# Up-projections of three feed-forward parts by seven products of halves in place of eight

## The chip, the cores and the metric

One core of one Trainium2 chip runs the kernel. The metric is the device time of one execution in microseconds (us), as the median of several runs. TensorE (PE) multiplies matrices, VectorE (DVE) and ScalarE (ACT) work on whole tiles, GpSimd (POOL) does smaller parts, and SyncE (SP) issues the transfers from memory.

## The reference

512 tokens of 1024 features pass through two blocks: a mixer of two attention branches, attention over a memory of 256 tokens, a feed-forward part with a gelu (stage ffa); then a retention part (ret), a feed-forward part with a silu (ffb), a stick-breaking attention (stk) and another feed-forward part (ffc). Each part adds to x. The change touches the feed-forward parts, all of width 2816:

```python
def conv_ffn(h, w_up, conv_w, conv_b, w_down):            # ffa
    u, g = jnp.split(h @ w_up, 2, axis=-1)
    u_pad = jnp.pad(u, ((0, 0), (CONV_WIDTH - 1, 0), (0, 0)))
    u = sum(conv_w[tap] * u_pad[:, tap:tap + S] for tap in range(CONV_WIDTH)) + conv_b
    return (jax.nn.gelu(u) * g) @ w_down

def _conv_ffn(h, w_up, conv_w, conv_b, w_down):           # ffb, ffc
    u = h @ w_up
    u = ...                       # the same causal convolution of width 3, over all 2 * 2816 columns
    gate, val = jnp.split(u, 2, axis=-1)
    return (jax.nn.silu(gate) * val) @ w_down

x = x + conv_ffn(rms_norm(x, ln_ffn_g), w_up, conv_w, conv_b, w_down)
```

## The kernel before

Activations lie transposed: x is eight tiles of 128 features x 512 tokens, all in SBUF. Every float32 factor is split into a high and a low part (`split`: ACT rounds the high part at L148, DVE subtracts to get the low one at L149), and a product is three matmuls, high by high, low by high, high by low (`mm3`, L175 to L177).

A feed-forward part (`ffn`) first scales and splits x (`norm_x`); the norm's factor of each token, rB, is applied when a product is read out of PSUM. Then come three blocks of 8, 8 and 6 pairs (`FF_PARTS`). A pair j is one u unit (columns j of the first half of w_up) and one g unit (the same columns of the second half). A unit is 128 output features: 1024 columns of weights, eight slices of 128 features with three matmuls of 512 tokens each, added up in one PSUM bank "pp" of six. `wload` fetches a unit by one DMA of 512 KB into one of two raw buffers wr and splits it into wh and wl, of which there are three each.

For each pair DVE reads u out of PSUM with the factor rB (L841), a convolution of three taps follows (ACT at L827, DVE at L828 and L829), ACT applies gelu or silu, DVE reads g (L846 in ffa; L852 in ffb and ffc, which convolve g too), multiplies (L847 or L854) and splits the result into mid (L855). After the pairs of a block, the down-projection of that block (`out_proj`, 24 matmuls a unit) adds eight tiles to x (L298), and in the last block of ffc `down_halves` does part of it by halves of the tokens, 256 columns a matmul, and the final norm.

Buffers of a stage come from a pool that the stage opens: 12 buffers wk of 512 columns for temporaries, 20 of mid. The library that records the kernel orders each engine's queue by a plan of its own; on the chip each engine runs its queue strictly in that order, and an instruction that waits holds up all behind it on its engine.

Of the kernel before, what the change touches and what calls it, by code (L numbers as in the profile page):

```python
# [65 lines left out]
def tile_blocks(ctx: ExitStack, tc: tile.TileContext, a: dict, out: bass.AP, dbg=None):  # L66
# [50 lines left out]


# [194 lines left out]
    def mixer():  # L313
        iw = a["w_in_fm"]
        keep = ExitStack()
        kp = sbpool("mix", keep)
        with stage("gla", {"pp": 4, "pa": 3, "ss": 1}, 5) as st:
# [32 lines left out]
            gl = sm.tile([P, NT, 24], F32, name="gl", bufs=1)  # L350
            al = sm.tile([P, NT, 16], F32, name="al", bufs=1)
# [8 lines left out]
            gates = sm.tile([P, NT, 24], F32, name="gates", bufs=1)  # L360
# [35 lines left out]
            for f in range(2):  # L396
# [219 lines left out]
        with stage("nsa", {"pp": 2, "s": 3, "pt": 2, "po": 1}, 2) as st:  # L616
# [52 lines left out]
            def values(kv, i, prs):  # L669
# [5 lines left out]
                for x, (b, o, n, v) in enumerate(blocks):  # L675
# [154 lines left out]

    def ffn(st, gname, up, down, second=None):
        h, rcol, rB, ahead = norm_x(gname, [a[up][i] for i in (0, NF, 1)])

        def up_unit(i):
            return ahead.pop(0) if ahead else fm_unit(wload(a[up][i]), h, KD)

        for part, (j0, nj) in enumerate(FF_PARTS):
            mid = []
            for j in range(j0, j0 + nj):
                u, y = wkt(), wkt()  # L840
                dve.tensor_mul(u, up_unit(j), rB)  # L841
                if second is None:
                    conv(y, u, "conv_w", "conv_b", NF, j)
                    act.activation(y, y, AF.Gelu_apprx_tanh)
                    g = wkt()
                    dve.tensor_mul(g, up_unit(NF + j), rB)  # L846
                    dve.tensor_mul(y, y, g)  # L847
                else:
                    conv(y, u, f"conv_w{second}", f"conv_b{second}", 2 * NF, j)
                    act.activation(y, y, AF.Silu)  # L850
                    u2, y2 = wkt(), wkt()
                    dve.tensor_mul(u2, up_unit(NF + j), rB)  # L852
                    conv(y2, u2, f"conv_w{second}", f"conv_b{second}", 2 * NF, NF + j)
                    dve.tensor_mul(y, y, y2)  # L854
                mid.append(split_new(y, st, "mid", 20))  # L855
# [4 lines left out]
    def down_halves(st, name, mid):  # L860
# [5 lines left out]
        us = [wload(a[name][m], tiles(st, "wd", 2, 2 * NHALF, F32R, w)) for m in range(m0, KD)]  # L866
# [7 lines left out]
        def finish(half, mid=None):  # L874
# [313 lines left out]
    with stage("ffa", {"pp": 6, "pa": 2}, 12) as st:  # L1188
        ffn(st, "ln_ffn", "w_up", "w_down")
# [4 lines left out]
    with stage("ffb", {"pp": 6, "pa": 2}, 12) as st:  # L1194
        ffn(st, "ffn_norm0", "up0", "down0", second=0)
# [4 lines left out]
    with stage("ffc", {"pp": 6, "pa": 2}, 12) as st:  # L1200
        ffn(st, "ffn_norm1", "up1", "down1", second=1)
# [149 lines left out]
```

## Time and profile before

| | |
|---|---|
| median of 3 runs | 2341.67 us (2338.39 to 2344.12) |
| the profiled execution, its span | 2338.12 us, 2336.3 us |
| granted TensorE clock, mean | 0.994 of full speed |
| PE busy (matmuls) | 2294.6 us, 98% of the span, 10872 |
| DVE busy | 1398.4 us, 60%, 2194 |
| ACT busy | 1021.6 us, 44%, 1662 |
| POOL busy | 194.0 us, 8%, 228 |
| one high part of a unit on ACT (L148, 128x1024) | 1044 ns on average |
| one high part of mid on ACT (L148, 128x512) | 631 ns on average |
| one weight unit from issue to landing | 3.2 us (median) |

The up-projection blocks, from the first u read out of PSUM (first block) or the last addition of the down-projection before (second and third) to the first addition of the block's own down-projection, in us from the trace:

| stage | first block, 8 pairs | second, 8 pairs | third, 6 pairs |
|---|---|---|---|
| ffa | 75.2 | 92.7 | 69.7 |
| ffb | 76.1 | 93.5 | 71.6 |
| ffc | 76.1 | 93.6 | 71.6 |

Busy time is a share of the span over stages with different limits. A matmul's own duration (some 0.39 us) is longer than the distance at which matmuls follow one another, since they overlap; a matmul's price is that distance. The same holds in a lesser degree on DVE.

### The profile page before, as it was taken

How to read it: one execution, taken by the hardware profiler on the slowest of the kernel's cores; microseconds unless marked ns; L12 is line 12 of the kernel's file. 1: busy time of each engine (PE TensorE's matmuls, PEld its weight loads, DVE VectorE, ACT ScalarE, POOL GpSimd, SP SyncE). 2: the span in 40 equal slices, each digit the busy share in tenths (PEclk: the TensorE clock that was granted, in tenths of full speed). 3: DMA queues.
4: the chain of work that ended last, by engine and by line, in shares of the span. 5: the costliest groups of instructions: out<-in, count | busy, mean ns of one | idle time of the engine just before them, and what ended most of it. 6: DMA issues, size and time to landing. Idle time of an engine off the chain costs nothing.

```text
span 2336.3 us, 28002 instructions
## 1 busy us (share of the span) xinstructions
PE 2294.6 (98%) x10872; PEld 1881.3 (81%) x10872; DVE 1398.4 (60%) x2194; ACT 1021.6 (44%) x1662; POOL 194.0 (8%) x228
## 2 busy tenths in 40 slices
PE   8999999999999999999999999999999999999997
PEld 7787778878888888888887788888888887888886
DVE  5457875457545356545454674746577886747465
ACT  4345763444323234423323442424477884424243
POOL 2001110101000003000000100000121101000002
PEclk9999999999999999999999999999999999999998
DMA  4221032312222223222222232222344322222222
GB/s 159 91 64 54 28 118 98 115 66 100 99 91 99 95 90 113 82 91 81 81 90 73 81 108 90 99 92 93 98 118 105 91 64 81 99 98 92 99 92 71
DMA packets 66054, 213.41 MB, mean 91 GB/s; under 512 B 7793, under 2 KB 10114, under 8 KB 65794
## 3 DMA queue, kind: packets, MB, share of 16 engines
q1 hardware_dynamic: 60802, 203.24, 26.2%
q0 software_dynamic: 5120, 8.39, 1.7%
q8 instruction: 85, 1.39, 0.2%
q14 instruction: 47, 0.39, 0.1%
HBM read 201.11 MB, written 2.10 MB: 87 GB/s over the span
## 4 chain that ended last, share of the span: by engine, by line
PE 91%; DVE 4%; ACT 2%; issue 1%; POOL 1%; DMA 0%; SPq 0%; DVEq 0%; POOLq 0%; ACTq 0%
PE pp L176 26%; PE pp L175 26%; PE pp L177 26%; PE po L682 1%; DVE wl L149 1%; DVE xl L268 1%; PE pt L678 1%; ACT pr L654 1%; PE po L1143 1%; PE pp L1050 1%; PE pp L1052 1%; PE pp L1051 1%; POOL pr L663 1%; DVE x L298 1%; PE pa L982 1%
## 5 line engine op out<-in xcount | busy, mean ns | idle before, releaser
L148 ACT ACTIVATE wh<-wr 128x1024 fp32r<-128x1024 f32 (+2 forms) x368 | 384.3, 1044 | 790.4 <-PE pp L176 623.2
L175 PE MATMUL pp<-xh,wh 128*128 128x512 f32 x1612 | 634.9, 394 | 3.0 <-ACT xh L267 2.8
L176 PE MATMUL pp<-xl,wh 128*128 128x512 f32 x1612 | 631.8, 392 | 3.6 <-DVE xl L268 3.6
L177 PE MATMUL pp<-xh,wl 128*128 128x512 f32 x1612 | 632.0, 392 | 0.0
L149 DVE TENSOR_TENSOR wl<-wr,wh 128x1024 fp32r<-128x1024 f32 (+2 forms) x368 | 452.4, 1229 | 209.3 <-ACT wh L148 182.8
L175 PEld LDWEIGHTS pp<-xh,wh 128*128 128x128 f32 x1612 | 303.8, 189 | 66.8 <-ACT xh L267 4.1
L176 PEld LDWEIGHTS pp<-xl,wh 128*128 128x128 f32 x1612 | 303.9, 189 | 66.3 <-DVE xl L268 5.5
L177 PEld LDWEIGHTS pp<-xh,wl 128*128 128x128 f32 x1612 | 303.7, 188 | 62.7 <-issue 0.9
L298 DVE TENSOR_TENSOR x<-x,pp 128x512 f32<-128x512 f32 x130 | 89.2, 686 | 244.4 <-PE pp L177 244.3
L175 PE MATMUL pp<-mid,wh 128*128 128x512 f32 x504 | 198.9, 396 | 0.0
L176 PE MATMUL pp<-mid,wh 128*128 128x512 f32 x504 | 198.6, 395 | 0.0
L177 PE MATMUL pp<-mid,wl 128*128 128x512 f32 x504 | 198.5, 395 | 0.0
L237 POOL TENSOR_TENSOR acc<-acc 128x512 f32<-128x512 f32 (+1 forms) x60 | 80.4, 1340 | 913.0 <-ACT acc L233 839.1
L176 PE MATMUL pp<-wl,xh 128*128 128x512 f32 (+1 forms) x320 | 122.3, 382 | 4.0 <-DVE wl L149 4.0
L175 PE MATMUL pp<-wh,xh 128*128 128x512 f32 (+1 forms) x320 | 121.4, 381 | 0.8 <-ACT wh L148 0.8
L177 PE MATMUL pp<-wh,xl 128*128 128x512 f32 (+1 forms) x320 | 121.3, 380 | 0.0
L175 PEld LDWEIGHTS pp<-mid,wh 128*128 128x128 f32 x504 | 94.4, 187 | 24.8 <-ACT mid L148 2.0
L176 PEld LDWEIGHTS pp<-mid,wh 128*128 128x128 f32 x504 | 94.4, 187 | 23.7 <-DVE mid L149 0.9
L177 PEld LDWEIGHTS pp<-mid,wl 128*128 128x128 f32 x504 | 94.4, 187 | 22.8
L148 ACT ACTIVATE mid<-wk 128x512 fp32r<-128x512 f32 x66 | 41.5, 631 | 124.4 <-DVE wk L854 108.8
L827 ACT ACTIVATE wk<-wk,vec 128x512 f32<-128x512 f32 x110 | 88.6, 809 | 6.5 <-DVE wk L841 5.2
L829 DVE SCALAR_TENSOR_TENSOR wk<-wk,vec 128x510 f32<-128x510 f32 x110 | 82.3, 750 | 3.6
(426 smaller groups left out, 3369.3 us busy)
## 6 DMA issues: line engine op xcount, KB each, us to landing
wr<-in_up SPq DMA_DIRECT2D x88, 512.0 KB, 3.2
wr<-in_w_up SPq DMA_DIRECT2D x44, 512.0 KB, 3.2
wr<-in_w_in_fm SPq DMA_DIRECT2D x32, 512.0 KB, 3.6
wr<-in_ret_vg SPq DMA_DIRECT2D x32, 512.0 KB, 3.2
wr<-in_down SPq DMA_DIRECT2D x32, 512.0 KB, 3.2
wr<-in_w_down SPq DMA_DIRECT2D x16, 512.0 KB, 3.2
wr<-in_ret_qk SPq DMA_DIRECT2D x16, 512.0 KB, 3.3
wr<-in_ret_out SPq DMA_DIRECT2D x16, 512.0 KB, 3.3
```

Source lines behind the costliest of these rows:

```text
L148: act.activation(hi, src, AF.Copy)
L149: dve.tensor_sub(lo, src, hi.bitcast(F32))
L175: pe.matmul(ps, sh, mh, start=first and i == 0, stop=False)
L176: pe.matmul(ps, sh, ml, start=False, stop=False)
L177: pe.matmul(ps, sl, mh, start=False, stop=last and i == n - 1)
L237: (dve if k == len(tiles) - 1 else pool).tensor_add(acc[:, :n], acc[:, :n], sq[:, :n])
L268: dve.scalar_tensor_tensor(lo, x, g, hi.bitcast(F32), op0=OP.mult, op1=OP.subtract)
L298: dve.tensor_add(xT[m], xT[m], ps)
L654: act.activation(dst, dst, AF.Exp, scale=-1.0, bias=nm[:, b:b + 1], accum_out=ss[:, g, b:b + 1])
L663: scaler(b).tensor_scalar(prs[g][b], prs[g][b], ss[:, g, b:b + 1], 1.0, op0=OP.mult, op1=OP.mult)
L827: act.activation(dst, src, AF.Identity, scale=V(wname, 2 * nw + j), bias=V(bname, j))
L829: dve.scalar_tensor_tensor(dst[:, 2:], src[:, :S - 2], V(wname, j), dst[:, 2:], op0=OP.mult, op1=OP.add)
```

## The change

Of each pair's 1024 x 256 weights and 1024 x 512 activations, the columns of weights (u and g), the features (first and second four slices) and the tokens (first and second 256) are halved. In place of eight products of halves, four for u and four for g, seven products of sums of halves are formed, each of 4 x 3 matmuls with 256 columns, and the results are put together from them. The first two pairs of each feed-forward part (`NPLAIN`) stay as they were. The sums of activations (t1 to t4) are formed once in a feed-forward part, those of weights (S1, S2, S4 in sa, S3 in the raw buffer of g) for every pair, two of them on POOL. Stage buffers change in size and number, and the pools are laid out with fillers.

```diff
+NPLAIN = 2
+HS = S // 2
...
+    def fill(pool_, n):
+        pool.memset(pool_.tile([P, n], F32, name="fill"), 0.0)
+    fill(sm_, 16)
...
-            gl = sm.tile([P, NT, 24], F32, name="gl", bufs=1)
+            gl = ms.tile([P, NT, 24], F32, name="gl", bufs=1)
...
+            fill(op, 120)
...
+        nrB, = tiles(st, "nrB", 1)
...
+        def plain(j):
+            ug = new_ug(st)
+            dve.tensor_mul(ug[:, 0, :], up_unit(j), rB)
+            dve.tensor_mul(ug[:, 1, :], up_unit(NF + j), rB)
+            return ug, 1.0
+
+        def half_sums():
+            out = []
+            for i in range(2):
+                out.append([st.tile([P, KD // 2, S], F32R, tag="tt", name="tt", bufs=4) for _ in range(2)])
+            for k in range(KD // 2):
+                y1, y2, t1, t2 = [wkt() for _ in range(4)]
+                act.activation(y1, xT[k], AF.Copy, scale=V(gname, k))
+                act.activation(y2, xT[k + 4], AF.Copy, scale=V(gname, k + 4))
+                dve.tensor_sub(t1[:, :HS], y1[:, :HS], y1[:, HS:])
+                dve.tensor_sub(t1[:, HS:], y2[:, HS:], y1[:, HS:])
+                split(out[0][0][:, k, :], out[0][1][:, k, :], t1)
+                dve.scalar_tensor_tensor(t2[:, :HS], t1[:, HS:], -1.0, y1[:, :HS], op0=OP.mult, op1=OP.subtract)
+                dve.scalar_tensor_tensor(t2[:, HS:], t2[:, :HS], -1.0, y2[:, :HS], op0=OP.mult, op1=OP.subtract)
+                split(out[1][0][:, k, :], out[1][1][:, k, :], t2)
...
+        def seven(j, ops):
+            ru, rg = [wpool.tile([P, UNIT], F32, tag="r", name="wr", bufs=NRAW) for _ in range(2)]
+            sync.dma_start(ru, a[up][j])
+            sync.dma_start(rg, a[up][NF + j])
+            k1, k2 = slice(0, S), slice(S, UNIT)
+            sa = st.tile([P, UNIT], F32, tag="sa", name="sa")
+            pool.tensor_add(sa[:, k1], rg[:, k1], rg[:, k2])
+            dve.tensor_add(sa[:, k2], sa[:, k1], ru[:, k1])
+            pool.tensor_add(rg[:, k1], rg[:, k1], ru[:, k1])
...
+            pu = parts(ru)
+            ps_ = parts(sa, st, ("sh", "sl"), 1)
+            dve.tensor_add(sa[:, k2], sa[:, k2], ru[:, k2])
+            pg = parts(rg)
+            p4 = parts(sa[:, k2], st, ("s4h", "s4l"), 1, S)
...
+            pa, pb, pc = [bank("pp")[:, :HS] for _ in range(3)]
...
+            product(pa, pu, 0, "11", True, True)
+            act.activation(g[:, h0], pa, AF.Copy)
+            product(pb, ps_, S, "t2", True, True)
+            dve.tensor_add(u[:, h1], pb, g[:, h0])
+            product(pc, ps_, 0, "t1", True, True)
+            dve.tensor_add(g[:, h1], pc, g[:, h0])
+            product(pa, pu, S, "21", False, True)
+            dve.tensor_mul(u[:, h0], pa, rB[:, h0])
+            product(pb, pg, 0, "t3", False, True)
+            dve.tensor_add(g[:, h1], pb, g[:, h1])
+            product(pc, p4, 0, "22", False, True)
+            dve.tensor_add(u[:, h1], pc, u[:, h1])
+            dve.tensor_mul(u[:, h1], u[:, h1], rB[:, h1])
+            product(pb, pg, S, "t4", False, True)
+            dve.tensor_add(g[:, h0], pb, g[:, h0])
+            dve.tensor_mul(g, g, nrB)
+            return ug
...
-                dve.tensor_mul(u, up_unit(j), rB)
+                    ug = seven(j, ops)
...
-                mid.append(split_new(y, st, "mid", 20))
+                mid.append(split_new(y, st, "mid", 18))
...
-    with stage("ffa", {"pp": 6, "pa": 2}, 12) as st:
+    with stage("ffa", {"pp": 6, "pa": 2}, 7) as st:
```

`parts` splits a source into its high and low part as `split` does; `product` is `mm3` over four slices with 256 columns; `down_halves` uses buffers of tags tt, ug and wk in place of its own.

DVE in the second block of ffb, before: one pair, from the reading of u (L841) to the split of mid (L149, mid). pp is PSUM, wr the raw weights, wh and wl their parts, wk a temporary.

```order
1273 L841 TENSOR_TENSOR wk<-pp,rB 128x512
1274 L149 TENSOR_TENSOR wl<-wr,wh 128x1024
1275 L828 SCALAR_TENSOR_TENSOR wk<-wk,vec 128x511
1276 L829 SCALAR_TENSOR_TENSOR wk<-wk,vec 128x510
1277 L852 TENSOR_TENSOR wk<-pp,rB 128x512
1278 L149 TENSOR_TENSOR wl<-wr,wh 128x1024
1279 L828 SCALAR_TENSOR_TENSOR wk<-wk,vec 128x511
1280 L829 SCALAR_TENSOR_TENSOR wk<-wk,vec 128x510
1281 L854 TENSOR_TENSOR wk<-wk 128x512
1282 L149 TENSOR_TENSOR mid<-wk,mid 128x512
```
DVE in the same block, after: the operations of the first part of a pair's time. ug holds u and g, sa the sums of weights, wsl the low part of S1 and S2; lines are those of the changed kernel, where the split is L157.

```order
1667 L914 TENSOR_TENSOR ug<-pp,ug 128x256
1668 L952 TENSOR_TENSOR wk<-wk 128x512
1669 L916 TENSOR_TENSOR ug<-pp,ug 128x256
1670 L918 TENSOR_TENSOR ug<-pp,rB 128x256
1671 L157 TENSOR_TENSOR mid<-wk,mid 128x512
1672 L920 TENSOR_TENSOR ug<-pp,ug 128x256
1673 L889 TENSOR_TENSOR sa<-sa,wr 128x512
1674 L157 TENSOR_TENSOR wl<-wr,wh 128x1024
1675 L922 TENSOR_TENSOR ug<-pp,ug 128x256
1676 L157 TENSOR_TENSOR wsl<-sa,wsh 128x1024
1677 L923 TENSOR_TENSOR ug<-ug,rB 128x256
1678 L925 TENSOR_TENSOR ug<-pp,ug 128x256
```
And the rest of that pair's time; ws4l is the low part of S4, L838 and L839 are the two convolution steps.

```order
1679 L899 TENSOR_TENSOR sa<-sa,wr 128x512
1680 L926 TENSOR_TENSOR ug<-ug,nrB 128x512
1681 L838 SCALAR_TENSOR_TENSOR wk<-ug,vec,wk 128x511
1682 L157 TENSOR_TENSOR wl<-wr,wh 128x1024
1683 L839 SCALAR_TENSOR_TENSOR wk<-ug,vec,wk 128x510
1684 L838 SCALAR_TENSOR_TENSOR wk<-ug,vec,wk 128x511
1685 L157 TENSOR_TENSOR ws4l<-sa,ws4h 128x512
1686 L839 SCALAR_TENSOR_TENSOR wk<-ug,vec,wk 128x510
```
Ten rows have become twenty: one split of 1024 columns more, the split of ws4l, two sums (L889, L899), seven operations of 256 columns in place of two readings of 512, and the scaling by nrB. The split of mid and the product (L952) belong to the pair before.

POOL at the norms before the memory attention and before ffa, and at the start of ret, before; L237 is the sum of squares of a norm, L210 a power, L904 a product of norm factors in ret.

```order
33 L210 TENSOR_TENSOR y<-v,mhalf 128x2
34 L237 TENSOR_TENSOR acc<-acc 128x512 x6
35 L210 TENSOR_TENSOR y<-v,mhalf 128x4
36 L237 TENSOR_TENSOR acc<-acc 128x512 x6
37 L210 TENSOR_TENSOR y<-v,mhalf 128x4
38 L904 TENSOR_TENSOR g_7095<-vec 128x1
```
POOL at the same two norms, and what follows them, after; L245 and L218 are those two lines now.

```order
36 L245 TENSOR_TENSOR acc<-acc 128x512 x6
37 L218 TENSOR_TENSOR y<-v,mhalf 128x4
38 L245 TENSOR_TENSOR acc<-acc 128x512 x6
39 L218 TENSOR_TENSOR y<-v,mhalf 128x4
40 L888 TENSOR_TENSOR sa<-wr 128x512
41 L890 TENSOR_TENSOR wr<-wr 128x512
42 L888 TENSOR_TENSOR sa<-wr 128x512
```
The norm's rows stand as they did; behind them 20 couples of additions (L888, L890), one for each pair of the new kind, follow in every feed-forward part.

## Rows read from the trace of the kernel before

**Rows 1.** Page, section 4: shares of the chain that ended last
```profile
PE 91%; DVE 4%; ACT 2%; issue 1%; POOL 1%; DMA 0%; SPq 0%; DVEq 0%; POOLq 0%; ACTq 0%
```

**Rows 2.** Windows: start:end, length, busy us (x) PE PEld DVE ACT POOL, PEclk, DMA
```profile
1447.70:1541.20 93.50, 93.50 (x412) 76.97 (x411) 65.65 (x82) 40.23 (x50) 0.00 (x0) 1.00 0.28 96
1579.70:1651.30 71.60, 71.60 (x315) 58.85 (x314) 49.10 (x63) 29.94 (x39) 0.00 (x0) 1.00 0.26 87
```

**Rows 3.** DVE timeline of ffb: start, us, line, operation, [wait <-releaser]
```profile
1332.35 0.68 DVE L841 TENSOR_TENSOR wk<-pp,rB 128x512 f32<-128x512 f32 x1
...
1408.47 0.69 DVE L298 TENSOR_TENSOR x<-x,pp 128x512 f32<-128x512 f32 x1 [0.82 <-PE pp L177]
...
1446.97 0.69 DVE L298 TENSOR_TENSOR x<-x,pp 128x512 f32<-128x512 f32 x1 [3.51 <-PE pp L177]
```

**Rows 4.** PE timeline, up-projection of ffb
```profile
1450.19 0.39 PE L175 MATMUL pp<-xh,wh 128*128 128x512 f32 x1
1450.42 0.39 PE L176 MATMUL pp<-xl,wh 128*128 128x512 f32 x1
```

**Rows 5.** PE timeline, memory projection and last down-projection
```profile
459.60 0.28 PE L175 MATMUL pp<-mm,wh 128*128 128x256 f32 x1
...
460.28 0.28 PE L175 MATMUL pp<-mm,wh 128*128 128x256 f32 x1
...
2301.03 0.39 PE L176 MATMUL pp<-mid,wh 128*128 128x512 f32 x1
...
2301.50 0.28 PE L175 MATMUL pp<-mid,wd 128*128 128x256 f32 x1
...
2302.08 0.28 PE L177 MATMUL pp<-mid,wd 128*128 128x256 f32 x1
...
2302.44 0.28 PE L177 MATMUL pp<-mid,wd 128*128 128x256 f32 x1
```

**Rows 6.** DVE timeline, three places
```profile
558.63 0.75 DVE L829 SCALAR_TENSOR_TENSOR wk<-wk,vec 128x510 f32<-128x510 f32 x1
559.29 0.74 DVE L828 SCALAR_TENSOR_TENSOR wk<-wk,vec 128x511 f32<-128x511 f32 x1
...
1353.36 0.68 DVE L841 TENSOR_TENSOR wk<-pp,rB 128x512 f32<-128x512 f32 x1
1353.96 1.21 DVE L149 TENSOR_TENSOR wl<-wr,wh 128x1024 fp32r<-128x1024 f32 x1
1355.10 0.74 DVE L828 SCALAR_TENSOR_TENSOR wk<-wk,vec 128x511 f32<-128x511 f32 x1
1355.87 0.75 DVE L829 SCALAR_TENSOR_TENSOR wk<-wk,vec 128x510 f32<-128x510 f32 x1
...
1799.04 0.42 DVE L1124 TENSOR_TENSOR S2l<-ab,S2h 128x256 fp32r<-128x256 f32 x1
1799.37 1.22 DVE L149 TENSOR_TENSOR wl<-wr,wh 128x1024 fp32r<-128x1024 f32 x1
```

**Rows 7.** Lines, 527.3 to 541.1 us: DVE, then POOL, then one DVE timeline row
```profile
L149 DVE TENSOR_TENSOR wl<-wr,wh 128x1024 fp32r<-128x1024 f32 x3 | 6.4, 2117 | 0.0
L268 DVE SCALAR_TENSOR_TENSOR xl<-x,vec,xh 128x512 fp32r<-128x512 f32 x6 | 6.2, 1064 | 0.0
L298 DVE TENSOR_TENSOR x<-x,pp 128x512 f32<-128x512 f32 x4 | 2.7, 676 | 0.0
...
L237 POOL TENSOR_TENSOR acc<-acc 128x512 f32<-128x512 f32 x6 | 10.5, 1757 | 51.1 <-issue 50.0 <-ACT acc L233 0.9
...
540.53 0.74 DVE L268 SCALAR_TENSOR_TENSOR xl<-x,vec,xh 128x512 fp32r<-128x512 f32 x1
```

**Rows 8.** Lines by form, POOL, whole span
```profile
L951 POOL TENSOR_TENSOR qk<-qk,wk 128x512 f32<-128x512 f32 x4 | 5.2, 1292 | 79.1 <-ACT wh L148 65.8 <-DVE wk L948 11.4 <-DVE qk L946 1.8
```

**Rows 9.** Windows: 120 to 130 us and 180 to 190 us
```profile
120.00:130.00 10.00, 10.00 (x38) 7.47 (x39) 6.61 (x13) 3.58 (x5) 0.00 (x0) 0.71 0.14 36
180.00:190.00 10.00, 7.45 (x39) 6.25 (x38) 5.96 (x10) 2.54 (x4) 0.00 (x0) 1.00 0.33 103
```

More of the change, by code (lines that the diff above doesn't have):

```diff
@@ L169, in wload, with mm3 @@
         return hi, lo
-    def mm3(ps, pairs, first=True, last=True):
+    def mm3(ps, pairs, first=True, last=True, **kw):
         n = len(pairs)
         for i, ((sh, sl), (mh, ml)) in enumerate(pairs):
-            pe.matmul(ps, sh, mh, start=first and i == 0, stop=False)
-            pe.matmul(ps, sh, ml, start=False, stop=False)
-            pe.matmul(ps, sl, mh, start=False, stop=last and i == n - 1)
+            pe.matmul(ps, sh, mh, start=first and i == 0, stop=False, **kw)
+            pe.matmul(ps, sh, ml, start=False, stop=False, **kw)
+            pe.matmul(ps, sl, mh, start=False, stop=last and i == n - 1, **kw)
     def fm_unit(unit, rhs, kt, ps=None, off=0, n=S):
@@ L315, in mixer @@
         keep = ExitStack()
+        ms = sbpool("mixs", keep)
         kp = sbpool("mix", keep)
@@ L839, in ffn @@
             for j in range(j0, j0 + nj):
-                u, y = wkt(), wkt()
-                dve.tensor_mul(u, up_unit(j), rB)
+                if j < NPLAIN:
+                    ug, _ = plain(j)
+                    if j == 0:
+                        dve.tensor_scalar(nrB, rB, -1.0, None, op0=OP.mult)
+                else:
+                    if ops is None:
+                        ops = half_sums()
+                    ug = seven(j, ops)
+                u, g = ug[:, 0, :], ug[:, 1, :]
+                y = wkt()
                 if second is None:
@@ L865, in down_halves @@
         w = len(mid) * P
-        us = [wload(a[name][m], tiles(st, "wd", 2, 2 * NHALF, F32R, w)) for m in range(m0, KD)]
+        wd = [st.tile([P, KD // 2, S], F32R, tag="tt", name="wd", bufs=4).rearrange("p k s -> p (k s)")
+              for _ in range(NHALF)]
+        us = [wload(a[name][m0 + i], (x[:, :w], x[:, UNIT:UNIT + w])) for i, x in enumerate(wd)]
         cols = [slice(i * n, i * n + n) for i in range(2)]
@@ L1193, in tile_blocks @@
     dump("xd")
-    with stage("ffb", {"pp": 6, "pa": 2}, 12) as st:
+    with stage("ffb", {"pp": 6, "pa": 2}, 7) as st:
         ffn(st, "ffn_norm0", "up0", "down0", second=0)
@@ L1199, in tile_blocks @@
     dump("xf")
-    with stage("ffc", {"pp": 6, "pa": 2}, 12) as st:
+    with stage("ffc", {"pp": 6, "pa": 2}, 7) as st:
         ffn(st, "ffn_norm1", "up1", "down1", second=1)
```

57 lines of the change are left out of this document (37 added, 20 removed).

## The prediction

> **What bounds the kernel now.** I read the page first, then the stretches of the feed-forward stages, then the queues of TensorE (PE) and VectorE (DVE) instruction by instruction. The page says that PE is busy for nearly the whole span, and that 91% of the chain that ended last is PE's [rows 1]. In the second block of stage ffb, from the last addition of one down-projection to the first of the next, PE is busy without a gap, DVE for 65.65 of 93.50 us, ScalarE (ACT) for 40.23 and GpSimd (POOL) not at all [rows 2]. DVE waits for PE there, and never the other way: an addition comes after 3.51 us of waiting for a product [rows 3]. So only fewer or faster matmuls can shorten these blocks, as long as DVE keeps up; its slack is 28 us in 93.50.
>
> PE's price there: matmuls of 512 columns start 0.227 us apart when both operands lie at multiples of 512 bytes [rows 4]. A pair (u unit and g unit) has 2 x 8 x 3 = 48 of them, 10.9 us; eight pairs and the first down-projection unit of 24 at 0.233 us [rows 5] give 92.7; the rows show 93.5.
>
> **The change part by part.** *PE.* A pair becomes 7 products of 4 x 3 matmuls of 256 columns, 84 in place of 48. Matmuls of 256 columns start 0.120 us apart in the last down-projection (three in 0.36), and 0.113 in the memory projection (six in 0.68) [rows 5]. So a pair costs 84 x 0.120 = 10.1 us (9.5 at 0.113): 12.5% fewer columns, but only 0.8 us less (1.4 at best). Over 60 such pairs (20 in each stage) that is 48 us (up to 84), if nothing else ends last.
>
> *DVE.* Instructions overlap a little, so what counts is the distance from one start to the next when nothing is waited for [rows 6]: 1.14 us for a split of 1024 columns, 0.60 for 512 (0.61 taken), 0.33 for 256, 0.77 for a convolution step that waits for the one before it, 0.66 for one that doesn't (0.72 taken). One pair now: 2 splits, 2 evictions, 2 convolution steps (4 in ffb and ffc), one product, one split of mid: 2.3 + 1.2 + 1.4 + 1.2 = 6.1 us, 7.6 in ffb and ffc. One pair after, by the order shown: 3 splits of 1024, one of 512 (ws4l), 2 sums (L889, L899), 7 operations of 256 columns (six on products, one scaling), the scaling by nrB, and the convolution, product and mid as before: 3.4 + 0.6 + 1.2 + 2.3 + 0.6 + 1.4 + 1.2 = 10.7 us, 12.2 in ffb and ffc. That already exceeds PE's 10.1. The cover of 28 us is gone: what is late next is DVE.
>
> *POOL.* Each pair adds two additions of 128x512 with both inputs in SBUF. POOL did six such in the norm before ffa while DVE had no gap. In that stretch DVE's three splits took 2117 ns on average, its six scaled splits 1064, and its four additions out of PSUM stayed at 676 [rows 7]. Undisturbed they are 1.21 and 0.74 us [rows 6, 7]. Excess: 3 x 0.91 + 6 x 0.32 = 4.6 us for six POOL additions, so 0.75 us of DVE's time for each. The bounds are 0, if they fall where DVE waits or reads PSUM, and 1.0, a scaled split's worst excess being about as long. I take 0.75, because in a pair DVE would have no gap either and four fifths of its time has both inputs in SBUF. The Trainium skill speaks against this part of the change more strongly: "SBUF — State Buffer", Who interferes with whom, says that a DVE instruction with two SBUF inputs and a GpSimd instruction reading SBUF exclude each other for a whole instruction. The trace agrees that only such DVE instructions are lengthened (676 ns against 2117). By the rule a POOL addition would cost DVE all of its undisturbed length, 1.29 us [rows 8], and the sum below would be some 50 us higher.
>
> *Blocks.* Counting DVE's instructions in the changed order from the first eviction of a block to the first down-projection addition, with the prices above (768 columns at 0.88, midway between 512 and 1024; the half sums' 256 columns at 0.37, an estimate a little over the row of 256; everything else of 512 at 0.61):
> - first block (2 plain pairs, 6 of the new kind, the half sums): 18 x 1.14 + 50 x 0.61 + 42 x 0.335 + 16 x 0.37 + 16 or 32 convolution steps = 82.5 us in ffa, 94.0 in ffb and ffc; 10 POOL additions, 7.5.
> - second (8 pairs): 23 x 1.14 + 44 x 0.61 + 56 x 0.335 + 16 or 32 steps = 83.3 and 94.9; 13 POOL additions, 9.8.
> - third (6 pairs): 14 x 1.14 + 3 x 0.88 + 32 x 0.61 + 42 x 0.335 + 12 or 24 steps = 60.8 and 69.5; 9 POOL additions, 6.8.
>
> Weights of the first pair of a block are prepared during the down-projection before it, where DVE has room, and are not in these counts. I add 2.9 us at the head of the second and third block (two products of 12 x 0.120 before the first eviction) and 1.4 at each tail (the last mid's split on ACT and the three matmuls that need it, estimated from the 0.63 of such a split on the page and 3 x 0.233).
> Before, the same stretches of ffb last 76.1, 93.5 and 71.6 us [rows 2, 3]; the table of blocks shows the same within 0.1 for ffc, and 75.2, 92.7 and 69.7 for ffa. After:
> - ffa: 91.4, 97.4, 71.9, so +16.2, +4.7, +2.2 = +23.
> - ffb and ffc: 102.9, 109.0, 80.6, so +26.8, +15.5, +9.0 = +51 each.
>
> Together +125 us. The remaining seven units of each down-projection are PE's at 24 matmuls each, before and after.
>
> *Buffers at multiples of 512 bytes.* By the built program's table of buffers mid moves from 448 bytes past such a multiple to 64 past one, as do tt, wsh and ws4h; only the buffers of the mixer's stages (k and v of its attention, pT, ons) reach a multiple. A 512-column matmul with an operand off it starts every 0.233 us against 0.227 [rows 4, 5]. So the down-projections gain nothing, and some 200 matmuls of the mixer gain 6 ns each: 1 us. Bounds: 0, and 1600 x 6 ns = 10 us, if it served the down-projections too.
>
> *At nothing:* the longer DMA waits of the two raw buffers (a weight lands 3.2 us after its issue, against a pair of 12 us or more); ACT, which gets 3 x 1.04 + 0.6 + 0.4 more or less as splits and one copy, under 8 us in a pair of 12; and the smaller number of wk buffers, since DVE's order already stands. If that cover fails, each costs a wait inside DVE's queue, which is in the upper end of the range.
>
> **Sum.** 2338.1 (the profiled execution) + 125 - 1 = 2462. That execution lay 3.5 us under the median of the runs, so I forecast 2465 us.
>
> **Rivals.**
> 1. *PE remains the bound and the change does what it says.* Then 60 x 0.8 to 60 x 1.4 us go from the median: 2258 to 2294 us. For it: DVE is only 70% busy in the block [rows 2]. Against it: even without POOL's share DVE needs 94.9 us in the second block of ffb, where PE had 93.5 with everything. It would need DVE's prices to be a fifth lower than each row shows; it decides from a DVE pair under 10.1 us. Chance 0.08.
> 2. *DVE is the bound, but POOL's additions cost it nothing*, because DVE stands waiting when they run: 125 less 3 x 24, with the convolution steps at 0.66 (220 of them, 13 us) and no tails (13 us): +27 to +53, so 2368 to 2395 us. For it: in a fixed order on DVE some waits are certain. Against it: a wait costs as much as it hides. Chance 0.14.
> 3. *DVE's queue also waits*: evictions that stand between splits hold up PE's next product in the same bank, and the split behind them in turn; sa, wsh and ws4h exist once. At 8% of DVE's 840 us in these blocks, and POOL additions at 1.0, it is +90 more: 2555 us. Nothing in the trace shows such a queue. Chance 0.10 for more than 2520.
> 4. *PE at half its clock.* Its granted clock was 0.71 of full in a stretch with PE busy for all of it, after short and partly idle work, and 1.00 in one where PE was busy only 7.45 of 10 us [rows 9]; so gaps alone did not lower it here. The Trainium skill ("TensorE: Matmul & The Clock Gate", Why this matters for your kernels) does warn that gaps between bursts of matmuls bring the slow level of 1.2 GHz back; the second of these rows shows gaps without it. At that level throughout, a pair would be 84 x 0.24 = 20 us and the time near 2338 + 60 x (20 - 11) = 2880. Chance 0.03.
> The forecast keeps 0.65, with its own range 2400 to 2520.
>
> **How the numbers follow.** The range must leave out no more than 0.2: rival 1 and the far part of rivals 3 and 4 stay outside, so 2368 (rival 2's low end) to 2540. About 0.3%, 7 us, is what a measurement of this kernel can tell from no change. Faster by more than that: rival 1, 0.08. Within it: the corner between rivals 1 and 2, 0.03. Slower: 0.89.
>
> **What would show it.** Right, if in the blocks of ffb and ffc DVE has hardly a gap while PE stands idle before the new products and waits for wl or wsl; if splits of 1024 columns have a mean above 1.6 us there; if a pair takes about 12 us in ffa and 13.7 in ffb; and if ffb and ffc lose about twice what ffa does. Wrong, if PE stays busy without gaps in these blocks, if a pair takes under 10.9 us, if POOL's additions leave the DVE splits at 1.2 us, or if matmuls on mid start 0.227 us apart.

## The result and the profile after

The changed kernel takes 2499.65 us (median of 4 runs, 2491.15 to 2502.3), against 2342.01 before: a ratio of 1.067, interval 1.0646 to 1.0694. The profiled span is 2499.7 us against 2336.3, 163.4 more.

The page's busy times and the chain that ended last, after:

```profile
PE 2317.1 (93%) x13032; PEld 1994.1 (80%) x13032; DVE 1772.3 (71%) x2869; ACT 1158.4 (46%) x1890; POOL 386.9 (15%) x350
...
PE 58%; DVE 21%; DMA 7%; POOL 5%; ACT 5%; issue 4%; POOLq 0%; SPq 0%; DVEq 0%; ACTq 0%
```
Against [rows 1], PE's share of the chain fell from 91% to 58%; DVE has 21%, DMA, POOL and ACT 17% together. PE's busy time hardly changed (2294.6 before). So PE alone no longer sets the end in these stages. The second block of ffa, and the second and third of ffb (columns as in [rows 2]):

```profile
691.99:800.95 108.96, 94.44 (x705) 90.41 (x704) 94.24 (x143) 46.92 (x64) 22.52 (x14) 0.95 0.29 87
1515.94:1631.15 115.21, 99.89 (x713) 94.10 (x712) 106.81 (x158) 53.37 (x72) 21.82 (x14) 0.94 0.26 82
1665.95:1753.92 87.97, 76.46 (x542) 71.22 (x541) 76.58 (x118) 39.21 (x54) 15.85 (x10) 0.94 0.24 76
```
The two blocks of ffb that [rows 2] shows went from 93.50 to 115.21 and from 71.60 to 87.97 us; PE has gaps in them now, DVE is busy for 93% and 87%, and POOL works. Here is the DVE queue of one pair in that second block (start, us, line, operation, in brackets what ended a wait), to the next pair's L889:

```profile
1577.78 1.45 DVE L889 TENSOR_TENSOR sa<-sa,wr 128x512 f32<-128x512 f32 x1
1579.15 1.21 DVE L157 TENSOR_TENSOR wl<-wr,wh 128x1024 fp32r<-128x1024 f32 x1
1580.29 0.41 DVE L922 TENSOR_TENSOR ug<-pp,ug 128x256 f32<-128x256 f32 x1
1580.74 1.22 DVE L157 TENSOR_TENSOR wsl<-sa,wsh 128x1024 fp32r<-128x1024 f32 x1
1581.89 0.42 DVE L923 TENSOR_TENSOR ug<-ug,rB 128x256 f32<-128x256 f32 x1
1582.22 0.42 DVE L925 TENSOR_TENSOR ug<-pp,ug 128x256 f32<-128x256 f32 x1
1582.56 0.68 DVE L899 TENSOR_TENSOR sa<-sa,wr 128x512 f32<-128x512 f32 x1
1583.16 0.68 DVE L926 TENSOR_TENSOR ug<-ug,nrB 128x512 f32<-128x512 f32 x1
1583.76 0.74 DVE L838 SCALAR_TENSOR_TENSOR wk<-ug,vec,wk 128x511 f32<-128x511 f32 x1
1584.42 1.22 DVE L157 TENSOR_TENSOR wl<-wr,wh 128x1024 fp32r<-128x1024 f32 x1
1585.56 0.74 DVE L839 SCALAR_TENSOR_TENSOR wk<-ug,vec,wk 128x510 f32<-128x510 f32 x1
1586.22 0.74 DVE L838 SCALAR_TENSOR_TENSOR wk<-ug,vec,wk 128x511 f32<-128x511 f32 x1
1586.88 0.68 DVE L157 TENSOR_TENSOR ws4l<-sa,ws4h 128x512 fp32r<-128x512 f32 x1
1587.48 0.74 DVE L839 SCALAR_TENSOR_TENSOR wk<-ug,vec,wk 128x510 f32<-128x510 f32 x1
1588.14 0.41 DVE L914 TENSOR_TENSOR ug<-pp,ug 128x256 f32<-128x256 f32 x1
1588.48 0.67 DVE L952 TENSOR_TENSOR wk<-wk 128x512 f32<-128x512 f32 x1
1589.08 0.41 DVE L916 TENSOR_TENSOR ug<-pp,ug 128x256 f32<-128x256 f32 x1
1589.41 0.41 DVE L918 TENSOR_TENSOR ug<-pp,rB 128x256 f32<-128x256 f32 x1
1589.85 1.54 DVE L157 TENSOR_TENSOR mid<-wk,mid 128x512 fp32r<-128x512 f32 x1
1591.31 0.41 DVE L920 TENSOR_TENSOR ug<-pp,ug 128x256 f32<-128x256 f32 x1
1591.65 1.43 DVE L889 TENSOR_TENSOR sa<-sa,wr 128x512 f32<-128x512 f32 x1
```
No row has a bracket: DVE waits for nothing, and the pair takes 1591.65 - 1577.78 = 13.87 us. Three instructions are longer than their kind: the sum L889 (1.45 and 1.43 where L899, of the same shape, takes 0.68) and the split of mid (1.54 where ws4l, of the same shape, takes 0.68). They lie beside POOL's additions, two for each pair, which run from 1575.67 to 1578.68 and from 1589.56 to 1592.53. The second couple:

```profile
1589.56 1.28 POOL L888 TENSOR_TENSOR sa<-wr 128x512 f32<-128x512 f32 x1 [10.88 <-DVE ug L916]
1590.92 1.61 POOL L890 TENSOR_TENSOR wr<-wr 128x512 f32<-128x512 f32 x1
```
By form over the whole second block (count, busy us, mean ns, idle time before and what ended it):

```profile
L157 DVE TENSOR_TENSOR wl<-wr,wh 128x1024 fp32r<-128x1024 f32 x17 | 22.9, 1345 | 0.2 <-ACT wh L156 0.2
...
L157 DVE TENSOR_TENSOR wsl<-sa,wsh 128x1024 fp32r<-128x1024 f32 x7 | 8.5, 1217 | 0.2
L889 DVE TENSOR_TENSOR sa<-sa,wr 128x512 f32<-128x512 f32 x7 | 8.2, 1174 | 3.1 <-POOL sa L888 3.1
L157 DVE TENSOR_TENSOR mid<-wk,mid 128x512 fp32r<-128x512 f32 x8 | 7.4, 926 | 2.3 <-ACT mid L156 2.2
```
A split wsl, which starts after POOL is through, keeps 1217 ns; L889 has 1174 and mid 926 on average. ffa is different. There the queues of SP, POOL and DVE read, around one pair (SP's rows are issues of transfers):

```profile
770.77 0.33 SPq L884 DMA_DIRECT2D wr<-in_w_up  x1
772.48 0.33 SPq L885 DMA_DIRECT2D wr<-in_w_up  x1
...
776.66 1.30 POOL L888 TENSOR_TENSOR sa<-wr 128x512 f32<-128x512 f32 x1 [11.72 <-DMA wr<-in_w_up]
778.03 1.80 POOL L890 TENSOR_TENSOR wr<-wr 128x512 f32<-128x512 f32 x1
...
777.99 0.69 DVE L889 TENSOR_TENSOR sa<-sa,wr 128x512 f32<-128x512 f32 x1 [1.24 <-POOL sa L888]
778.60 0.42 DVE L922 TENSOR_TENSOR ug<-pp,ug 128x256 f32<-128x256 f32 x1
780.95 1.23 DVE L157 TENSOR_TENSOR wl<-wr,wh 128x1024 fp32r<-128x1024 f32 x1 [1.94 <-ACT wh L156]
```
The transfers of the next raw weights are issued at 770.77 and 772.48, when the raw buffers of u and g come free; POOL's first addition has waited for the second of them and runs from 776.66 to 777.96; DVE's L889 stands waiting for 1.24 us until 777.99. Then POOL's second addition runs until 779.83, ACT rounds its result, and DVE's next split waits 1.94 us for ACT. Over the whole run DVE waited so for POOL 26 times, 43.9 us in all, 5.1 at most:

```profile
DVE sa L889 <- POOL sa L888: 43.9, 26, 5.1
```

### The profile page after: what moved, and what is told of

Same layout as the page of the kernel before. It is cut to its first block, busy times and chain, and to the rows that moved or that the text cites. A ratio compares the mean times of both kernels' runs of the same rounds, so it can differ in the third digit from the quotient of the medians.

```text
span 2499.7 us, 33644 instructions
## 1 busy us (share of the span) xinstructions
PE 2317.1 (93%) x13032; PEld 1994.1 (80%) x13032; DVE 1772.3 (71%) x2869; ACT 1158.4 (46%) x1890; POOL 386.9 (15%) x350
## 4 chain that ended last, share of the span: by engine, by line
PE 58%; DVE 21%; DMA 7%; POOL 5%; ACT 5%; issue 4%; POOLq 0%; SPq 0%; DVEq 0%; ACTq 0%
PE pp L183 15%; PE pp L184 15%; PE pp L185 15%; DVE wl L157 6%; DMA wr<-in_up 4%; POOL sa L888 2%; DVE wsl L157 2%; ACT wh L156 2%; DVE wk L838 2%; DMA wr<-in_w_up 2%; POOL wr L890 2%; DVE wk L839 1%; DVE sa L899 1%; PE po L691 1%; PE pt L687 1%
## 5 line engine op out<-in xcount | busy, mean ns | idle before, releaser
L157 DVE TENSOR_TENSOR wl<-wr,wh 128x1024 fp32r<-128x1024 f32 (+2 forms) x368 | 477.4, 1297 | 189.3 <-ACT wh L156 176.2
L183 PE MATMUL pp<-xh,wh 128*128 128x512 f32 (+1 forms) x1132 | 407.1, 360 | 57.1 <-ACT ug L912 29.6
L185 PE MATMUL pp<-xh,wl 128*128 128x512 f32 (+1 forms) x1132 | 402.4, 355 | 17.6 <-DVE wl L157 17.6
L184 PE MATMUL pp<-xl,wh 128*128 128x512 f32 (+1 forms) x1132 | 400.3, 354 | 3.6 <-DVE xl L276 3.6
L888 POOL TENSOR_TENSOR sa<-wr 128x512 f32<-128x512 f32 x60 | 85.1, 1418 | 902.3 <-DMA wr<-in_up 520.7
L183 PE MATMUL pp<-mid,wh 128*128 128x512 f32 x504 | 197.6, 394 | 10.1 <-ACT wh L156 8.9
L183 PE MATMUL pp<-tt,wh 128*128 128x256 f32 x480 | 146.1, 304 | 38.9 <-DVE ug L914 22.0
L183 PE MATMUL pp<-tt,wsh 128*128 128x256 f32 x480 | 140.5, 296 | 16.4 <-ACT tt L156 9.0
L184 PE MATMUL pp<-tt,wsh 128*128 128x256 f32 x480 | 139.9, 293 | 3.4 <-DVE tt L157 3.2
L185 PE MATMUL pp<-tt,wl 128*128 128x256 f32 x480 | 140.1, 292 | 0.0
L184 PE MATMUL pp<-tt,wh 128*128 128x256 f32 x480 | 139.8, 291 | 0.0
L185 PE MATMUL pp<-tt,wsl 128*128 128x256 f32 x480 | 137.2, 292 | 0.0
L183 PEld LDWEIGHTS pp<-tt,wh 128*128 128x128 f32 x480 | 95.6, 199 | 51.7 <-DVE ug L914 30.5
L245 POOL TENSOR_TENSOR acc<-acc 128x512 f32<-128x512 f32 (+1 forms) x60 | 83.3, 1389 | 310.8 <-ACT acc L241 244.7
L837 ACT ACTIVATE wk<-ug,vec 128x512 f32<-128x512 f32 x110 | 89.0, 812 | 80.6 <-DVE ug L923 66.1
```

The lines of the kernel that those rows point to most:

```text
L157: dve.tensor_sub(lo, src, hi.bitcast(F32))
L183: pe.matmul(ps, sh, mh, start=first and i == 0, stop=False, **kw)
L184: pe.matmul(ps, sh, ml, start=False, stop=False, **kw)
L185: pe.matmul(ps, sl, mh, start=False, stop=last and i == n - 1, **kw)
L245: (dve if k == len(tiles) - 1 else pool).tensor_add(acc[:, :n], acc[:, :n], sq[:, :n])
L837: act.activation(dst, src, AF.Identity, scale=V(wname, 2 * nw + j), bias=V(bname, j))
```

## The experiments

Theory A: the blocks are bound by DVE, which has more work, is lengthened by POOL's additions, and loses some time waiting for fresh weights. Theory B: two raw buffers close a loop (use up, fetch, add, split) that sets the pace. Theory C: TensorE's clock falls in the gaps and sets it. The kernel before was timed beside each run, at 2339 to 2342 us, so a difference of 2 or 3 us between two runs says nothing. The library plans the queues anew for each edit: in the second block of ffb DVE has the change's order in e10, nearly the same in e1, a partly different one in e3 and a different one in e2, so what the last two show holds the edit and the new order together.

**No POOL additions (e1).**

```diff
-            pool.tensor_add(sa[:, k1], rg[:, k1], rg[:, k2])
+            act.activation(sa[:, k1], rg[:, k1], AF.Copy)
...
-            pool.tensor_add(rg[:, k1], rg[:, k1], ru[:, k1])
```

> Leaves out the two POOL additions of each pair: the first half of sa is a copy of the raw g weights made by ACT (0.63 us), and S3 is the raw g weights alone; every split, sum on DVE and product stays. Theory A (the blocks are bound by DVE, which POOL's additions lengthen): the 73 us by which DVE's instructions in the nine blocks are longer than their undisturbed selves go, and most of the 24 us in which DVE waits for the first POOL addition, so 2400 to 2430 us, with DVE busy over 90% of the second block of ffb. Theory B (two raw buffers: a pair cannot start before the raw weights of the one before are used up, fetched and added): the loop loses only POOL's 1.3 us a pair and DVE's lengthening was hidden in it, so 2440 to 2480. Theory C (TensorE at half its clock after gaps sets the pace): within 15 us of 2500.

2399.49 us (ratio to before 1.0258, 1.0242 to 1.0273): 100 less than the change. The second blocks of ffa and ffb:

```profile
680.47:773.09 92.62, 89.93 (x705) 86.15 (x704) 86.51 (x143) 50.01 (x71) 0.00 (x0) 1.00 0.31 98
1470.86:1572.82 101.96, 93.68 (x713) 88.98 (x712) 96.55 (x159) 56.43 (x79) 0.00 (x0) 0.98 0.29 89
```
DVE is busy for 93% and 95% of them, and DVE's lengthening is gone. That is half a microsecond under A's range and 40 under B's. 100 us for 120 additions is 0.83 each, but not all of it is lengthening: in the nine blocks of the three stages (up-projection blocks as in the table of before) DVE's lengthening fell from 72 to 6 us, and the time in which DVE has no work from 90 to 54.

**The additions on DVE (e2).**

```diff
-            pool.tensor_add(sa[:, k1], rg[:, k1], rg[:, k2])
+            dve.tensor_add(sa[:, k1], rg[:, k1], rg[:, k2])
...
-            pool.tensor_add(rg[:, k1], rg[:, k1], ru[:, k1])
+            dve.tensor_add(rg[:, k1], rg[:, k1], ru[:, k1])
```

> The two additions of raw weights run on DVE in place of POOL. Theory A: DVE gets 60 x 2 x 0.60 = 72 us of work and loses 73 us of lengthening, and waits less for POOL: 2470 to 2500 us. Theory B: two cross-engine steps fewer in the loop through the raw buffers, and DVE has room: 2420 to 2460. If POOL's additions cost DVE nothing at all (rival 2 of the prediction), 2550 to 2575.

2482.52 us (1.061, 1.0594 to 1.0626), as A has it. The second block of ffb:

```profile
1511.49:1622.19 110.70, 91.73 (x694) 86.70 (x693) 104.64 (x172) 51.76 (x71) 0.00 (x0) 0.98 0.27 81
```
DVE does 14 instructions more there than in the change and the block is 4.5 us shorter: handing the two additions to POOL saved no time. In the nine blocks DVE's own work rises by 60 us, and its lengthening falls by 67.

**POOL's additions doubled (e10).**

```diff
+            for _ in range(2):
+                scr = st.tile([P, S], F32, tag="scr", name="scr", bufs=1)
+                pool.tensor_add(scr, ru[:, k1], ru[:, k2])
```

> Doubles POOL's additions: behind the two of each pair it does two more of the same size on the raw u weights, into a buffer that nobody reads; the result is unchanged. Nothing waits for them but the release of the raw u buffer. Theory A (each POOL addition costs DVE 0.55 to 0.85 us by lengthening an instruction of DVE's): 120 more cost 120 x 0.55 to 120 x 0.85 = 66 to 102 us, less what falls into DVE's idle time (79 us in the nine blocks, a tenth of their length): 2555 to 2595 us, DVE's excess in the second block of ffb rising from 11 to about 20 us. If POOL's additions cost only by their own latency in the loop: 2500 to 2520.

2575.94 us (1.1019, 1.1 to 1.1037), inside A's range: 76 us for 120 more additions, 0.64 each. The second block of ffb:

```profile
1551.55:1677.16 125.61, 103.52 (x713) 96.66 (x712) 114.63 (x158) 53.84 (x72) 45.64 (x28) 0.92 0.24 76
```
And three groups of DVE by form over the whole span:

```profile
L838 DVE SCALAR_TENSOR_TENSOR wk<-ug,vec,wk 128x511 f32<-128x511 f32 x110 | 109.0, 993 | 2.5 <-ACT wk L837 2.4
L839 DVE SCALAR_TENSOR_TENSOR wk<-ug,vec,wk 128x510 f32<-128x510 f32 x110 | 106.1, 967 | 0.7
...
L157 DVE TENSOR_TENSOR wsl<-sa,wsh 128x1024 fp32r<-128x1024 f32 x60 | 72.9, 1214 | 2.4 <-ACT wsh L156 2.0
```
In the change the convolution steps L838 and L839 have means of 811 and 816 ns, here 993 and 967, while wsl, at 1214, is as it was: whatever DVE instruction with two SBUF inputs lies beside POOL pays. In the nine blocks the lengthening rose from 72 to 140 us for 97 more additions there, 0.70 each, as in the change itself (72 us for 102, 0.71). In the kernel's time an addition is worth 0.64 us when added and 0.83 when removed; the larger figure holds the waits that go with it.

**A third raw buffer (e3).**

```diff
+        turn = [0]
...
+        def raw3(st):
+            turn[0] += 1
+            if turn[0] % 3 == 0:
+                return st.tile([P, UNIT], F32, tag="r3", name="wr", bufs=1)
+            return wpool.tile([P, UNIT], F32, tag="r", name="wr", bufs=NRAW)
...
-            ru, rg = [wpool.tile([P, UNIT], F32, tag="r", name="wr", bufs=NRAW) for _ in range(2)]
+            ru, rg = [raw3(st) for _ in range(2)]
...
-    with stage("ffa", {"pp": 6, "pa": 2}, 7) as st:
+    with stage("ffa", {"pp": 6, "pa": 2}, 6) as st:
...
```

> A third raw buffer for the seven-product pairs (4 KB more, paid for by 6 wk buffers in place of 7), so that weights of the next pair can be fetched and added earlier. Theory A: only DVE's waits for the first POOL addition and for ACT's rounding of fresh weights can go, some 24 + 14 us, most of them in ffa: 2465 to 2500 us. Theory B: the pace falls to DVE's own, 10.7 us a pair in ffa and 12.2 in the others plus POOL's share: 2400 to 2440, ffa gaining most. Theory C: 2490 to 2505.

2475.42 us (1.0583, 1.0566 to 1.0601): 24 less than the change. The second block of ffa:

```profile
690.94:789.43 98.49, 91.00 (x697) 85.63 (x697) 95.21 (x142) 46.60 (x63) 21.62 (x14) 1.00 0.29 93
```
And DVE's wait for POOL's first addition over the span (L897 here):

```profile
DVE sa L897 <- POOL sa L896: 26.8, 15, 4.9
```
The wait is down from 43.9 to 26.8 us, that block fell from 108.96 to 98.49 us and DVE is busy for 97% of it. The time is inside A's range and 35 us over B's. So the raw buffers did cost something, but they were not the bound: the three blocks of ffa fell by 21 us together, those of ffb by 7 and of ffc by 4.

**Both (e7).** The edits of e1 and e3 together, on the ground that B would then have nothing left to wait for.

> e1 and e3 together: no POOL additions (S1's first sum is a copy by ACT, S3 is the raw g weights) and a third raw buffer. In e1 DVE is idle for 50 us in the nine blocks together, of which heads and tails hold some 25. Theory A: the buffer can give back only a part of the rest: 2380 to 2398 us, DVE's own instructions being the floor. Theory B: 2340 to 2370, since the loop through the raw buffers is then the last wait.

2388.37 us (1.0209, 1.0194 to 1.0224). With neither POOL nor a short supply of raw weights the kernel is still 49 us slower than before. DVE's own work in the nine blocks is 746 us here, more than the 720 that these blocks took before; A holds and B falls.

**Weights prepared once in a block (e4).**

```diff
+        kept = {}
...
+        def weights(j):
+            block = [j0 <= j < j0 + nj for j0, nj in FF_PARTS].index(True)
+            if block not in kept:
+                kept[block] = prepare(j)
+            return kept[block]
...
+            pu, ps_, pg, p4 = weights(j)
```

> The weights of the seven-product pairs are fetched, added and split once in each block, for its first such pair, and every later pair of the block multiplies with those: leaves out 51 of the 60 fetches, sums and splits, keeps all matmuls and everything behind them. It shows what the seven products alone are worth. Theory A: DVE has 7 to 8.5 us of work in a pair, PE sets the pace with 84 matmuls: at 0.120 us 10.1 a pair, so 2338 - 60 x 0.8 + 12 for the three first blocks' heads and the half sums = 2290 to 2310 us. If the 256-column matmuls keep the shorter step of 0.113, 2260 to 2280. Theory C: gaps behind the products lower the clock and it stays above 2338.

2300.90 us (0.9837, 0.9822 to 0.9852). The second block of ffb:

```profile
1437.39:1524.74 87.35, 87.35 (x708) 85.44 (x707) 63.68 (x117) 28.00 (x44) 0.00 (x0) 1.00 0.07 24
```
PE has no gap, the clock is at its full level, and DVE's scaling by nrB comes every 9.88 us, 84 matmuls at 0.118. The time is inside A's range. Seven products of 256 columns are worth 1.0 us of PE's time a pair, if nobody has to prepare their operands; with the half sums and the heads of the blocks 39 us are left in all. C falls with this and with the runs above.

**The layout alone (e5), and at multiples of 512 (e6).**

```diff
-NPLAIN = 2
+NPLAIN = 99
```

> The changed kernel with all pairs by eight products (NPLAIN 99): its pools, fillers and buffer counts alone. mid lies 64 bytes past a multiple of 512, as in the changed kernel. If the layout is what made the mixer 4 us, ret 1.3 us and the matmuls on mid 4 ns (0.233 to 0.229) shorter in the changed kernel's trace: 2339.7 - 4 - 1 - 1584 x 0.004 = 2326 to 2332 us. As the prediction had it (mid gains nothing, 1 us in the mixer): 2337 to 2341. If fewer wk and mid buffers cost waits: above 2342.

```diff
-NPLAIN = 2
+NPLAIN = 99
...
-    fill(sm_, 16)
...
+        fill(ms, 16)
```

> As e5, but the 64-byte filler stands in the mixer's pool, so that the buffers of all stages (mid, wk, the operands of ret and stk) lie at multiples of 512. If a matmul's step is 0.227 us only with both operands at such a multiple: mid's matmuls go from 0.229 to 0.227, and those of ret and stk gain likewise, 2000 x 2 to 4 ns = 4 to 8 us below e5, 2318 to 2327 us. If 64 bytes past the multiple is as good: within 2 us of e5.

2332.38 us (0.9967, 0.9955 to 0.9978) and 2327.26 (0.9945, 0.9933 to 0.9958). Each is a little faster than the kernel before, by 0.3% and 0.5% with intervals that leave out 1, and the second is the fastest of all that keep the whole computation. The first lies 0.4 us above the range for a gain in mixer, ret and mid, the second 0.3 us above its own; within 2 us of each other they are not. Its matmuls on mid, in the down-projection of ffb's second block:

```profile
1544.85 0.39 PE L182 MATMUL pp<-mid,wh 128*128 128x512 f32 x1
1545.08 0.39 PE L183 MATMUL pp<-mid,wh 128*128 128x512 f32 x1
1545.30 0.39 PE L184 MATMUL pp<-mid,wl 128*128 128x512 f32 x1
1545.53 0.39 PE L182 MATMUL pp<-mid,wh 128*128 128x512 f32 x1
1545.76 0.39 PE L183 MATMUL pp<-mid,wh 128*128 128x512 f32 x1
```
Four steps in 0.91 us. The medians over 1512 matmuls on mid are 0.233 (mid 448 bytes past a multiple of 512), 0.229 (64 past) and 0.227 (at one). 1512 x 4 ns is 6 us and 1512 x 6 ns is 9 us, which is what the stretch from the last of the mixer's additions to x (448.24 before) to the fourth of ffc's last block (2301.70) lost: 6.3 and 8.7. The mixer itself gained nothing: its first addition to x comes at 409.04 before, 408.98 and 410.60 here.

**The change with that layout (e8).**

```diff
-    fill(sm_, 16)
...
+        fill(ms, 16)
```

> The changed kernel with the filler as in e6. The matmuls on mid gain 1584 x 2 ns; the 256-column matmuls have shown 0.113 to 0.120 us whatever their operands' place, and DVE bounds the blocks: 2490 to 2499 us. If tt and the split weights at multiples of 512 shortened the 256-column matmuls to 0.113, nothing more would follow, since DVE sets the pace.

2493.55 us (1.0658, 1.0643 to 1.0672), inside the range. That is 6 us under the change, but the kernel before was timed 3 us lower beside it, and the two intervals overlap. The medians are 0.227 us for a matmul on mid and 0.120 for the 256-column matmuls on the half sums: the latter gained nothing.

**Some pairs only (e9).** Seven products where DVE has slack, with e6's layout. The half sums are formed in the second block here, from an x that the first down-projection has changed; the instructions are the same as formed in time.

```diff
-NPLAIN = 2
+EVERY = {None: 2, 0: 3, 1: 3}
...
-                if j < NPLAIN:
+                if j < FF_PARTS[1][0] or j % EVERY[second]:
```

> The layout of e6, and seven products only in the second and third blocks, for every second pair in ffa and every third in ffb and ffc (17 pairs in all), where DVE has slack: in ffa DVE's work is then (10.7 + 1.5 + 6.1) / 2 = 9.2 us a pair, in the others (13.7 + 2 x 7.6) / 3 = 9.6, under PE's 10.5. Theory A: 17 x 0.8 to 17 x 1.0 us under e6, less up to 8 us for the half sums where DVE has no room: from 17 below e6 to 5 below. If a pair's DVE queue holds up PE whatever the mean load: 5 to 30 us above e6.

2357.24 us (1.007, 1.0056 to 1.0085): 30 above e6, so A's 5 to 17 below is missed, and the other case, 5 to 30 above, is met at its upper end. The second block of ffb, and 15 us of it:

```profile
1445.24:1552.77 107.53, 98.43 (x528) 84.93 (x527) 92.38 (x137) 54.05 (x75) 9.85 (x6) 0.95 0.25 84
1490.00:1505.00 15.00, 10.55 (x53) 9.26 (x52) 14.08 (x18) 6.19 (x9) 2.77 (x2) 0.77 0.14 38
```
That block is 14 us longer than in e6 (93.51), with DVE busy for only 86% of it, but in the second row DVE has 14.08 of 15 us and PE 10.55. The load is not spread: half sums, and the three splits and two sums of a new pair, stand in front of the readings of the plain pairs in DVE's queue, PE stands idle, and its clock falls. In ffa, where DVE's load is less, the second and third block did get 1.3 and 1.5 us shorter (91.14 and 68.18, against 92.48 and 69.72). A mean of DVE's load over three pairs does not tell whether it fits. A queue with the half sums and the sums of weights spread out was not run.

## Why the prediction was right, and which sizes were off

The time lay 35 us above the forecast and inside its range, and what bounds the blocks was named rightly. In part it is luck that it came so near: the nine blocks took 65 us more than the sum has, and the rest of the span 27 us less than before, where the sum has 1. Term by term, in us, with POOL's share counted from the trace of after as what DVE's instructions took beyond the shortest tenth of their kind's durations, and DVE's own work as its busy time less that:

| | predicted | measured |
|---|---|---|
| DVE's own work in the nine blocks | 743 | 748 |
| lengthened by POOL | 72 | 72 |
| DVE without work, heads and tails included | 30 | 90 |
| nine blocks together (before: 720) | 845 | 910 |
| change of the nine blocks | +125 | +190 |
| the rest of the down-projections, to the end | 0 | -29 |
| from the addition before each stage to its first reading | 0 | +8 |
| elsewhere | -1 | -6 |
| change of the span | +124 | +163 |

- *What bounds.* "what is late next is DVE" held: removing POOL's part, moving it and doubling it moved the time as DVE's queue says. Pairs took 13.6 us in ffb (seven distances in the second block, predicted 13.7), 12.9 in ffa (about 12).
- *PE.* 84 x 0.120 was near: e4 has 9.88 us a pair, between the 9.5 and 10.1 of the prediction.
- *POOL.* 0.75 us an addition was taken for 96 in the blocks; 102 fell there, at 0.71 each. The term is right within 2% because the two errors cancel. Where it falls was wrong: the splits of weights were to have a mean above 1.6 us in ffb, and have 1.345; L889 and the split of mid took their share.
- *At nothing*, and this is the step that failed: "the longer DMA waits of the two raw buffers" were costed at zero, because a transfer of 3.2 us looked short against a pair of 12. But a raw buffer is free only when its last sum and split are done, late in the pair, and then transfer, POOL's addition and DVE's L889 follow in a row, with all of DVE's queue behind L889. A third buffer gave 24 us back, with DVE's time without work in the blocks down from 90 to 65.
- *DVE without work, by cause.* Of the 90 us, 27 are waits for POOL's first addition (17 of them at the six heads of the second and third blocks) and 13 for ACT's rounding of fresh weights: 40 for that chain. Another 13 are the tails, as predicted. The 17 us at the heads are what the prediction had there too, but by luck: it had two products as their cause, and L889 waits 2.6 to 3.1 us for POOL at each. The rest stood at nothing: 19 us of waits for products, and 14 for ACT's other roundings and activations (4 are gaps too short to be put down to anything); of ACT the prediction had the load alone, which did leave room (53.4 of 115.2 us in ffb's second block). Half of the excess over 30 is in ffa: its three blocks' +23 became +53, where those of ffb and ffc have +67 and +71 for +51, so they did not lose twice what ffa did.
- *The down-projections* were held unchanged, but fall by 26 us from the first addition on, and the end by 3. 5.5 us of the 26 are the layout (e5). In the rest the boundary moved: PE's changed order has 41 matmuls on mid before the first addition of ffb's second block, where it had 28, while the last mid is late. So 13 matmuls, 3 us, now fall inside the block, where DVE sets the end.
- *Heads of the stages.* In ffb, between norm and first reading, L889 of the first new pair stands in DVE's queue and waits 5.1 us for POOL. It was not in the sum: 8 us over the three stages. Without POOL's additions (e1) the three stretches are as long as before, within 0.1 us.
- *Layout.* "The down-projections gain nothing" was wrong by 4 ns a matmul: 64 bytes past a multiple is not as 448 past one. The upper bound, 10 us, is near what the full multiple gives (8.7 us in e6).
- *Rivals.* 1 needed a DVE pair under 10.1 us; e4 makes one, by leaving the work out, and lands at 2301, between the rival's time and before. 2 falls, since the time fell by 100 us without POOL's additions. 3 is where the miss lies, in kind: DVE's queue waits, for fresh weights first of all and for products second. 4 came in part: the clock's mean is 0.968.

## What to carry to other kernels

A product scheme with fewer multiplications is paid in sums, splits and readings; price those on the engine that does them, instruction by instruction, before counting columns, and compare with what PE takes for the same pair. Work handed to POOL is not off a busy DVE's account: here the same two additions cost no more on DVE itself. Where a stage fetches into two raw buffers and something else works on the raw data first, the wait is the whole chain from the last use to the first result, and not the transfer alone. An engine's mean slack is no room in an in-order queue: look where in the queue the added work stands, and who is behind it.

## What the runs showed of the hardware

- Matmuls of 512 columns start every 0.233 (before), 0.229 (e5) or 0.227 us (e6) in the median as the moving operand mid lies 448, 64 or 0 bytes past a multiple of 512. The offsets are those of the built program's table of buffers. Matmuls of 256 columns on half sums and weight sums gain nothing from the multiple: medians of 0.116 to 0.120 at 64, 0.120 at 0. Which of the offsets between would do is open.
- TensorE's clock fell after gaps. In ffb's second block, after a stretch in which PE was busy 2.85 of 5 us and stood idle for 2.2 us at its end:

```profile
1556.00:1561.00 5.00, 2.85 (x24) 2.64 (x23) 5.00 (x9) 2.31 (x4) 0.00 (x0) 1.00 0.50 143
1561.00:1566.00 5.00, 4.94 (x29) 4.94 (x30) 4.83 (x7) 0.53 (x2) 3.42 (x2) 0.66 0.16 66
```
The granted clock is 1.00 in the first stretch and 0.66 in the second, so part of it ran at 1.2 GHz in place of 2.4; in e4 the same block, without gaps, has 1.00 throughout. The Trainium skill ("TensorE: Matmul & The Clock Gate", Why this matters for your kernels) warns that gaps between bursts of matmuls bring the slow level back, and these rows agree, where [rows 9] alone did not. What it cost here was not measured apart. DVE set the pace, and its waits for products inside the nine blocks are 19 us here and 18 in e1, where the clock's mean is 0.98 in place of 0.97. The 4 us by which the mixer ended earlier in the profile of after can't be put down to the layout: e5, with the same layout, has none of it. The clock from 100 to 150 us was 0.90 before, 0.93 after and 0.86 in e5; whether that is all of the 4 us is open.
- A DVE instruction with two SBUF inputs that starts while one of POOL's additions runs finishes behind it, in 84 of 85 cases. In the couple shown the first addition ends at 1590.84, and the split of mid at 1591.39; the second ends at 1592.53, and L889 at 1593.08: each 0.55 us later, where it takes 0.68 undisturbed. The reading of PSUM between them (L920, 0.41) is not lengthened. The addition waits too: L890 starts at 1590.92, while the split of mid runs, ends 1.14 us behind it and is 1.61 long where L888 has 1.28. Over the whole run of the change, 85 such instructions start while one of the 120 additions runs; 84 of them end behind that addition by their own length less 0 to 0.2 us. The 85 together are 0.81 us longer than undisturbed on average, 69 us in all. The other 35 additions met none. The 64 instructions that read PSUM beside an addition are longer by 0.02 us at most. So an addition costs DVE what is left of it when such an instruction comes to its turn, and nothing otherwise. These rows agree with the rule of the Trainium skill that the prediction cites ("SBUF — State Buffer", Who interferes with whom). The prediction's reading of it, that each addition would cost its whole 1.29 us, does not: the runs show 0.70 to 0.71 on average in the blocks.
